# Gates of the last 128 tokens: three bf16 products per token in place of one fp32 product

## The chip, the cores and the metric

The kernel runs on one core of a Trainium2 chip. The metric is the device time of one execution in microseconds (us), taken as the median over several runs. Engines are named as the profile names them: PE is TensorE's matmul side and PEld its weight loads, DVE is VectorE, ACT is ScalarE, POOL is GpSimd, SP is SyncE, which here only issues transfers (SPq).

## What is computed

The program is a decoder trunk of four layers over 256 tokens of width 1024, all in fp32. Each layer has an attention mixer (sliding window, dilated, latent, sliding window again) and then an expert mixer, called PEER, with a normalisation behind each. PEER is where the change lies. Cut to what matters, it is this:

```
q     = x @ w_q                                   # 8 heads, two halves of 128
sc    = q . keys                                  # 128 keys per half
best, idx = top 16 of the sums of the top 16 of both halves   # idx = 128*row + column
gate  = softmax(best)                             # 16 experts per head, 8 heads
h     = gelu(x . u[idx]);  y = sum(gate * h * v[idx])
```

There are 128*128 experts, and each token uses 128 of them. The kernel does not gather rows of u and v. It computes gelu(x . u) for all 16384 experts as dense products, multiplies with a gate matrix that is zero for experts that a token did not choose, and multiplies with all of v.

## The kernel before

A layer's PEER stage has four parts, each bound to the stream of weights that SP loads in chunks of 512 KB (`raw`), ACT rounds to a high part (`hi`) and DVE, now and then POOL, subtracts to a low part (`lo`). Every large product is three fp32r products, hi*zh, lo*zh and hi*zl.

- Scores: `peer_scores` computes the queries and the key scores of 256 tokens on PE.
- Top-k: `topk_gen` runs as a side program on DVE, a few instructions per chunk, for tokens 0 to 127 first and then for tokens 128 to 255.
- The u phase: 128 chunks of u (index j), 24 products of 256 columns each on PE (`hp`, L141), followed by a gelu on ACT into G.
- The v phase: 123 chunks of v and five more at the end, 12 products of 512 columns each (L151 to L155), which read G after it has been multiplied by the gates and split.

The gates come by two ways. For tokens 0 to 127, POOL scatters them with 128 indirect transfers per layer (`scatter`, L957, `gates<-gt`) into a gate matrix in DRAM. SP fetches it piece by piece (L1022, `gt<-gates`) at the start of the v phase, after the last scatter has landed, and DVE multiplies it into G (L1031, `gated`). For tokens 128 to 255 the gate matrix is made on the chip. `topk_gen` ends with three fp32 transposes (L910) that turn row number, column number and gate value of each chosen expert into `tab`, with the 128 experts on the partitions and the tokens along the free axis. Then `weights_gen` takes the tokens in 32 units of four. For a unit, DVE builds in the tile `wk` a one-hot matrix over rows and one over columns (L925, both in one instruction of 1024 elements) and multiplies the second by the gate values (L927, 512 elements). PE multiplies the two for each token (L941, fp32, 128 x 128 x 128), which gives that token's 128 x 128 gate matrix in a bank of PSUM (`y0` to `y3`). `keep` then stores it into G (ACT, L999) or multiplies it into what stands there already (DVE, L1006).

The order of PE, DVE, ACT and SP is the order in which the code is written; POOL runs its scatters on its own. `pace` lets the side program run along the u phase: every chunk j gives it a budget, each `yield` takes the number behind it from the budget, and a unit of `weights_gen` costs 1. The units start when `topk_gen` has ended, with a budget per chunk of 35/(125 - j), so that they are spread over the rest of the u phase. Within a unit's step, the next unit's builds are issued on DVE ahead of this unit's products on PE.

The tile `wk` has two buffers and `sm` (the small PSUM tile that the transposes write) two.

Of the kernel before, what the change touches and what calls it, by code (L numbers as in the profile page):

```python
# [11 lines left out]
F32 = mybir.dt.float32  # L12
F32R = mybir.dt.float32r
BF = mybir.dt.bfloat16
# [3 lines left out]
OP = mybir.AluOpType  # L18
# [26 lines left out]
class Kernel:  # L45
# [453 lines left out]
    def swa(self, j):  # L499
        nc = self.nc  # L500
        self.turned = 1
        kT, vT = self.carve(T), self.carve(T)
        v = self.carve(2, 128)
        qTs = self.ring(8, T)
        pts = self.ring(4, 384)
        ptTs = self.ring(4, 384)
        st = self.ring(2, 6, 4)
        ost = self.carve(8, T)
        sk = self.carve(16)
        sinks = self.a["sinks"]  # L510
        nc.sync.dma_start(sk, bass.AP(tensor=sinks.tensor, offset=sinks.offset + 16 * j, ap=[[0, 128], [1, 16]]))
        self.xproj(kT, True)
        self.xproj(vT, True)
        self.vtrans(vT, v)
        bias = self.aux[:, 0:4096].rearrange("p (h s) -> p h s", h=16)

        def sink(c, s):
            sv = s.rearrange("p a (e t) -> p a e t", e=2)
            skc = sk[:, 2 * c:2 * c + 2][:, :, None].to_broadcast([128, 2, 2])
            nc.vector.tensor_add(sv[:, 2], sv[:, 0], skc)  # L520
            nc.vector.tensor_scalar(s[:, 2], s[:, 2], 88.0, None, op0=OP.min)
            nc.scalar.activation(s[:, 3], s[:, 2], AF.Exp)

        def gains(it):
            s = it["s"]
            nc.vector.tensor_add(s[:, 4], s[:, 3], s[:, 1])
            nc.vector.reciprocal(s[:, 5], s[:, 4])

        items = [dict(c=c, heads=(c, c + 8), s=st[c % 2], ix=[(0, 1), (2, 3)], pt=pts[2 * (c % 2):][:2],
                      ptT=ptTs[2 * (c % 2):][:2], v=v, scale=HD ** -0.5, bias=lambda h: bias[:, h, :],  # L530
                      terms=lambda e, c=c: [(qTs[c], kT, slice(64 * e, 64 * e + 64))]) for c in range(8)]
        ahead = 1 if self.started else 2
        for c in range(ahead):
            self.xproj(qTs[c])
        if not self.started:
            first = self.layers[0]
            todo = self.to_mask
            self.load_biases(first, nc.sync, slice(2, 4))
            self.to_mask = todo
            self.load_norms(first - 1, nc.sync)  # L540

        def after(c):
            sink(c, st[c % 2])

        def before(c):
            if ahead <= c + 1 < 8:
                self.xproj(qTs[c + 1])
            if c == 5 and not self.started:
                self.started = True

        if not self.started:
            self.mask_biases(2)
        self.pipeline(items, gains, ost, before, lambda c: self.mask_biases(2) if c else None, after)

    def dilated(self, j):
# [234 lines left out]
    def topk_gen(self, ids, val, tab, ready):  # L790


        nc = self.nc
        V = nc.vector
        svs, sis = self.ring(2, 16, 16), self.ring(2, 16, 16, dt=U32)
# [7 lines left out]
        stk = self.carve(3, 128)  # L803
# [15 lines left out]
        for t in range(2):  # L819
# [33 lines left out]
            shape = [128, 4, 16, 16]  # L853
# [54 lines left out]
        p = self.small((128, 4, 128))  # L908
        for q in range(3):
            nc.tensor.transpose(p[:, q, :], stk[:, q, :], self.ident)  # L910
        V.tensor_copy(tab, p[:, 0:3, :])
        yield 0.55

    def weights_gen(self, tab, keep):


        nc = self.nc
        V = nc.vector
        shape = [128, 2, 4, 128]
        units = {}  # L920

        def build(u):
            ts = slice(124 - 4 * u, 128 - 4 * u)
            ab = self.misc.tile(shape, F32, name="wk", bufs=2)
            V.tensor_tensor(ab, self.iota[:, None, None, :].to_broadcast(shape),  # L925
                            tab[:, 0:2, ts][:, :, :, None].to_broadcast(shape), op=OP.is_equal)
            V.tensor_mul(ab[:, 1], ab[:, 1], tab[:, 2, ts][:, :, None].to_broadcast([128, 4, 128]))  # L927
            units[u] = ab

        build(0)  # L930
        yield 1
        kept, due = None, None
        for u in range(34):
            if u + 1 < 32:
                build(u + 1)
            p = None
            if u < 32:
                p = self.ps.tile([128, 4, 128], F32, name=f"y{u % 4}", bufs=1)
                ab = units.pop(u)
                for k in range(4):  # L940
                    nc.tensor.matmul(p[:, k, :], ab[:, 0, k, :], ab[:, 1, k, :], start=True, stop=True)  # L941
            if due is not None:
                due()
            due = keep(256 - 4 * u, kept.rearrange("p t j -> p j t")) if kept is not None else None
            kept = p
            yield 1
# [26 lines left out]
    def peer(self, i, turn):  # L973
        nc = self.nc
        self.new_work()
        iv = self.misc.tile([128, 2, 128], F32, name="gt", bufs=2)
        ids, val = iv[:, 0, :].bitcast(I32), iv[:, 1, :]
        tab = self.misc.tile([128, 3, 128], F32, name="tab", bufs=1)
        self.sc = self.carve(2, 16, 128)
        self.sc_ready, self.paced = 0, 0.0  # L980
        sent = []
# [34 lines left out]
        rows = self.gates[i].rearrange("(n b p c) o -> n p b (c o)", b=2, p=128, c=128)  # L1016
# [64 lines left out]
        for j in range(n):  # L1081
# [12 lines left out]
            if j in (68, 71, 74, 77):  # L1094
                k = (j - 68) // 3
                self.load_norms(i, nc.sync, slice(k, k + 1))
            if j in (80, 83, 86, 89):
                k = (j - 80) // 3
# [79 lines left out]
    def setup(self):  # L1178
        nc, a = self.nc, self.a
        self.ident = self.misc.tile([128, 128], F32, name="ident", bufs=1)  # L1180
        nc.scalar.dma_start(self.ident, a["ident"])
        self.x = self.misc.tile([128, 2, 1024], F32, name="x", bufs=1)
        self.new_work()
        rb, oh, rr = self.carve(16), self.carve(RW), self.carve(RW)
        for t in range(2):
            nc.sync.dma_start(self.x[:, t, :], a["x"][t * 128:t * 128 + 128, :])
            if t == 0:
                nc.sync.dma_start(oh[0:32], a["bucket"])
        nc.scalar.dma_start(rb[0:32], a["rel_bias"])
        for _ in range(2):  # L1190
            self._load()
        self.eps = self.misc.tile([128, 4], F32, name="eps", bufs=1)
        nc.vector.memset(self.eps[:, 0:1], LN_EPS)
        nc.vector.memset(self.eps[:, 1:2], RMS_EPS)
        p = self.small()
        nc.tensor.matmul(p[0:16, 0:RW], rb[0:32], oh[0:32], start=True, stop=True)
        nc.scalar.activation(rr[0:16], p[0:16, 0:RW], AF.Copy, scale=HD ** 0.5)
        self.relb = self.dram.tile([16, RW], F32, name="relb")
        nc.sync.dma_start(self.relb, rr[0:16])
        self.prefetch()  # L1200
        self.new_z()
        for t in range(2):
            self.turn_lo(self.turn_hi(t, [self.asmall() for _ in range(2)]))
            self.split_to(0)
        self.prefetch()
        self.masks = self.misc.tile([128, 1024], F32, name="masks", bufs=1)
        nc.sync.dma_start(self.masks, a["masks"])
        self.new_aux()
        self.load_biases(self.layers[0], nc.sync, slice(0, 2))
        self.zero = self.misc.tile([128, 128], F32, name="zero", bufs=1)  # L1210
        nc.vector.memset(self.zero, 0.0)
        self.steps = self.misc.tile([128, 33], F32, name="steps", bufs=1)
        nc.gpsimd.dma_start(self.steps, a["steps"])
        self.iota = self.misc.tile([128, 128], F32, name="iota", bufs=1)
        nc.gpsimd.dma_start(self.iota, a["iota"])

    def build(self):
        tc = self.tc
# [114 lines left out]
```

## Time and profile before

| | |
|---|---|
| median of three runs | 3824.62 us (3823.56 to 3825.99) |
| the profiled execution | 3826.61 us, its span 3824.8 us, mean granted TensorE clock 0.999 |
| PE busy | 3792.5 us, 99% of the span |
| PEld, DVE, ACT, POOL busy | 91%, 74%, 49%, 29% |
| POOL's scatters, L957 | 1017.6 us in 512 instructions |

The span runs from the first to the last instruction; the time of the execution is 1.8 us longer. A duration of one PE or PEld instruction in the profile is longer than its share of the engine's time, since the instructions overlap: the share is read from the distance of two starts. Each fp32 product of L941 stands in the profile as two MATMUL records, so a unit of four products is eight records.

### The profile page before, as it was taken

The numbers are of one execution on the slowest core, as the hardware profiler recorded it, in microseconds if no ns is written. First come the engines' busy times: TensorE is split into PE (matmuls) and PEld (weight loads), VectorE is DVE, ScalarE is ACT, GpSimd is POOL, SyncE is SP. The second block draws the span as 40 slices with busy tenths as digits, with TensorE's granted clock in tenths as the row PEclk, the third lists the DMA queues.
The fourth block names the chain that finished last, engine by engine and source line by source line (L and its number), as shares of the span: only waits on it lengthen the run. The fifth ranks groups of instructions, "written<-read, shape, count | busy, mean of one in ns | idle before, by whom it ended". The sixth has DMA issues, their size and how long they took to land. (4 is left out here: it accounts for less than half of the span.)

```text
span 3824.8 us, 67261 instructions
## 1 busy us (share of the span) xinstructions
PE 3792.5 (99%) x25652; PEld 3468.1 (91%) x25652; DVE 2826.6 (74%) x5914; ACT 1878.3 (49%) x3400; POOL 1091.9 (29%) x548
## 2 busy tenths in 40 slices
PE   8999999999999999999999999999999999999999
PEld 7999998888998999988887999998888899998887
DVE  7787776676667887766667788776677788776666
ACT  5544444545554544455555444444555554445554
POOL 0158750000000188720000148860000128780000
PEclk9999999999999999999999999999999999999999
DMA  7667777775444577777762567778775456666665
GB/s 236 201 183 180 174 207 239 246 242 163 142 138 147 171 186 178 176 226 240 250 211 99 168 182 180 177 185 246 245 249 164 144 182 179 160 158 215 215 226 176
DMA packets 400996, 735.35 MB, mean 192 GB/s; under 512 B 102608, under 2 KB 240400, under 8 KB 400160
## 3 DMA queue, kind: packets, MB, share of 16 engines
q1 hardware_dynamic: 326688, 730.60, 59.4%
q0 software_dynamic: 73792, 0.38, 5.5%
q8 instruction: 201, 3.29, 0.3%
q14 instruction: 123, 1.01, 0.1%
q10 hardware_dynamic: 192, 0.07, 0.0%
HBM read 696.01 MB, written 34.89 MB: 191 GB/s over the span
## 5 line engine op out<-in xcount | busy, mean ns | idle before, releaser
L97 DVE TENSOR_TENSOR lo<-raw,hi 128x1024 fp32r<-128x1024 f32 x1182 | 1444.2, 1223 | 595.2 <-ACT hi L91 591.9
L91 ACT ACTIVATE hi<-raw 128x1024 fp32r<-128x1024 f32 x1212 | 1271.2, 1050 | 32.9 <-DMA raw<-in_peer_v 21.2
L957 POOL DMA_INDIRECT gates<-gt x512 | 1017.6, 1988 | 485.0 <-DVE G L808 247.7
L141 PE MATMUL hp<-zh,hi 128*128 128x256 f32 x5312 | 764.0, 286 | 1.6 <-ACT zh L242 0.7
L141 PE MATMUL hp<-zh,lo 128*128 128x256 f32 x5312 | 746.4, 283 | 0.0
L141 PE MATMUL hp<-zl,hi 128*128 128x256 f32 x5312 | 746.1, 283 | 0.0
L141 PEld LDWEIGHTS hp<-zh,hi 128*128 128x128 f32 x5312 | 682.7, 192 | 7.6 <-issue 4.5
L141 PEld LDWEIGHTS hp<-zh,lo 128*128 128x128 f32 x5312 | 685.9, 192 | 0.0
L141 PEld LDWEIGHTS hp<-zl,hi 128*128 128x128 f32 x5312 | 685.8, 192 | 0.0
L155 PE MATMUL y<-hi,wk 128*128 128x512 f32 x2004 | 624.9, 393 | 1.5 <-DVE wk L1037 1.3
L153 PE MATMUL y<-lo,wk 128*128 128x512 f32 x2004 | 623.1, 392 | 0.0
L151 PE MATMUL y<-hi,wk 128*128 128x512 f32 x2004 | 621.1, 390 | 0.0
L97 POOL TENSOR_TENSOR lo<-raw,hi 128x1024 fp32r<-128x1024 f32 x30 | 72.7, 2424 | 1871.8 <-ACT hi L91 1871.8
L1051 ACT ACTIVATE G<-hp 128x256 f32<-128x256 f32 (+26 forms) x512 | 182.6, 357 | 836.8 <-PE hp L141 825.9
L1036 ACT ACTIVATE wk<-G 128x256 fp32r<-128x256 f32 x492 | 205.9, 418 | 656.9 <-issue 625.1
L155 PEld LDWEIGHTS y<-hi,wk 128*128 128x128 f32 x2004 | 375.9, 188 | 85.5 <-DVE wk L1037 2.1
L151 PEld LDWEIGHTS y<-hi,wk 128*128 128x128 f32 x2004 | 375.8, 188 | 84.2 <-ACT wk L1113 0.3
L153 PEld LDWEIGHTS y<-lo,wk 128*128 128x128 f32 x2004 | 376.5, 188 | 80.1
L1037 DVE TENSOR_TENSOR wk<-G,wk 128x256 fp32r<-128x256 f32 x492 | 208.8, 424 | 263.3 <-ACT wk L1036 263.2
L427 ACT ACTIVATE G<-hp 128x256 f32<-128x256 f32 x156 | 59.7, 382 | 203.4 <-PE hp L141 195.9
L925 DVE TENSOR_TENSOR wk<-iota,tab 128x1024 f32<-128x1024 f32 x128 | 156.1, 1219 | 0.0
L1031 DVE TENSOR_TENSOR G<-G,gt 128x128 f32<-128x128 f32 x512 | 144.3, 284 | 7.6 <-DMA gt<-gates 7.4
(202 smaller groups left out, 2611.7 us busy)
## 6 DMA issues: line engine op xcount, KB each, us to landing
raw<-in_peer_u SPq DMA_DIRECT2D x512, 512.0 KB
raw<-in_peer_v SPq DMA_DIRECT2D x512, 512.0 KB
raw<-in_dil_w SPq DMA_DIRECT2D x72, 512.0 KB
gates<-zero SPq DMA_DIRECT2D x256, 128.0 KB
raw<-in_peer_wq SPq DMA_DIRECT2D x64, 512.0 KB
gt<-gates SPq DMA_DIRECT2D x256, 128.0 KB
raw<-in_swa_w SPq DMA_DIRECT2D x20, 512.0 KB
G<-in_lnp SPq DMA_DIRECT2D x16, 512.0 KB
```

Source lines behind the costliest of these rows:

```text
L91: nc.scalar.activation(h[:, :w], r[:, :w], AF.Copy)
L97: eng.tensor_sub(lo[:, :w], r[:, :w], h.bitcast(F32)[:, :w])
L141: mm(ps, w[:, k, :], z[:, k0 + k, :], start=(p == 0 and k == 0), stop=(p == 2 and k == nk - 1))
L151: mm(ps[t][b][:, :s.stop - s.start], zh[:, ts], hi[:, s], start=first, stop=False)
L153: mm(ps[t][b][:, :s.stop - s.start], zh[:, ts], lo[:, s], start=False, stop=False)
L155: mm(ps[t][b][:, :s.stop - s.start], zl[:, ts], hi[:, s], start=False, stop=last)
L925: V.tensor_tensor(ab, self.iota[:, None, None, :].to_broadcast(shape), tab[:, 0:2, ts][:, :, :, None].to_broadcast(shape), op=OP.is_equal)
L957: ins = self.nc.gpsimd.indirect_dma_start(self.gates[i], IndirectOffsetOnAxis(ap=ids[:, k:k + 1], axis=0), val[:, k:k + 1], None, compute_ ...
L1031: nc.vector.tensor_mul(g, g, gts[j // 2][:, j % 2, :])
L1036: nc.scalar.activation(gz[:, 0, :], g, AF.Copy)
L1037: nc.vector.tensor_sub(gz[:, 1, :], g, gz.bitcast(F32)[:, 0, :])
L1051: nc.scalar.activation(g[:, 0:td], ps[:, 0:td], AF.Gelu)
```

## The change

The one-hot matrices become bf16. The gate value is split into three bf16 parts, which together hold the fp32 value: `topk_gen` gains two subtractions and two casts for that, each with a `yield` of 0.28, and `tab` becomes bf16 with five rows. Row numbers and column numbers are whole numbers below 128. A unit's builds are now three DVE instructions. One compares a new constant `iota4` (each number 0 to 127 four times) with the column numbers, 512 elements in the order column, token. One multiplies that by the three parts of the gate, 1536 elements. One builds the rows' one-hot, 512 elements in the order token, row. PE computes three bf16 products per token, which add up in PSUM; the moving operand is read with a step of four elements, the stationary one without a step. `iota4` is made by one DVE instruction in the first layer's mixer.

```
+                nc.vector.tensor_copy(self.iota4, self.iota[:, :, None].to_broadcast([128, 128, 4]))
                 self.started = True
...
-        V.tensor_copy(tab, p[:, 0:3, :])
+        V.tensor_copy(tab[:, 0:3], p[:, 0:3, :])
         yield 0.55
+        left = stk[:, 0, :]
+        V.tensor_sub(left, p[:, 2, :], tab[:, 2])
+        yield 0.28
+        V.tensor_copy(tab[:, 3], left)
+        yield 0.28
+        V.tensor_sub(left, left, tab[:, 3])
+        yield 0.28
+        V.tensor_copy(tab[:, 4], left)
+        yield 0.28
...
-            ab = self.misc.tile(shape, F32, name="wk", bufs=2)
-            V.tensor_tensor(ab, self.iota[:, None, None, :].to_broadcast(shape),
-                            tab[:, 0:2, ts][:, :, :, None].to_broadcast(shape), op=OP.is_equal)
-            V.tensor_mul(ab[:, 1], ab[:, 1], tab[:, 2, ts][:, :, None].to_broadcast([128, 4, 128]))
-            units[u] = ab
+            ab = self.misc.tile([128, 2048], BF, name="wk", bufs=2)
+            rows = ab[:, 0:512].rearrange("p (k i) -> p k i", k=4)
+            cols = ab[:, 512:2048].rearrange("p (q j k) -> p q j k", q=3, k=4)
+            V.tensor_tensor(cols[:, 2], self.iota4, tab[:, 1, ts][:, None, :].to_broadcast([128, 128, 4]),
+                            op=OP.is_equal)
+            V.tensor_mul(cols, cols[:, 2][:, None].to_broadcast([128, 3, 128, 4]),
+                         tab[:, 2:5, ts][:, :, None, :].to_broadcast([128, 3, 128, 4]))
+            V.tensor_tensor(rows, self.iota4[:, :, 0][:, None, :].to_broadcast([128, 4, 128]),
+                            tab[:, 0, ts][:, :, None].to_broadcast([128, 4, 128]), op=OP.is_equal)
+            units[u] = rows, cols
...
-                    nc.tensor.matmul(p[:, k, :], ab[:, 0, k, :], ab[:, 1, k, :], start=True, stop=True)
+                    for q in range(3):
+                        nc.tensor.matmul(p[:, k, :], rows[:, k, :], cols[:, q, :, k], start=q == 0, stop=q == 2)
...
-        tab = self.misc.tile([128, 3, 128], F32, name="tab", bufs=1)
+        tab = self.misc.tile([128, 5, 128], BF, name="tab", bufs=1)
```

On PE, in the first layer, around the first unit of four tokens (L941, tile `y_4218`), the kernel before has this order; `hp` is the u phase's product:

```order
L141 MATMUL hp<-zl,hi 128x256 x8
L141 MATMUL hp<-zh,hi 128x256 x8
L141 MATMUL hp<-zh,lo 128x256 x8
L141 MATMUL hp<-zl,hi 128x256 x8
L941 MATMUL y_4218<-wk 128x128 x4
L141 MATMUL hp<-zh,hi 128x256 x8
```

At the same place, one chunk later, the changed kernel has this (L957 is now the line of the products, the tile is `y_4259`):

```order
L141 MATMUL hp<-zl,hi 128x256 x8
L957 LDWEIGHTS wk
L957 MATMUL y_4259<-wk 128x128
L957 LDWEIGHTS wk
L957 MATMUL y_4259<-wk 128x128
```

Four fp32 products, which load their weights themselves, became twelve pairs of a load and a product. Counted over a layer, the 32 units stood behind chunks 2, 4, 6, 8, 9 and so on to 58 after the transposes, and stand now behind chunks 3, 5, 7, 9, 10 and so on to 58.

On DVE, in the first layer, between the copy of the transposes (L911) and the second unit's builds, before; `lo` is the low part of a weight chunk:

```order
L911 COPY tab<-sm 128x384
L97 TENSOR_TENSOR lo<-raw,hi 128x1024
L925 TENSOR_TENSOR wk<-iota,tab 128x1024
L927 TENSOR_TENSOR wk<-wk,tab 128x512
L97 TENSOR_TENSOR lo<-raw,hi 128x1024
L925 TENSOR_TENSOR wk<-iota,tab 128x1024
L927 TENSOR_TENSOR wk<-wk,tab 128x512
```

And now, where the copy is L913, the parts of the gate L916 to L922 and the three builds L937, L939 and L941:

```order
L913 CAST tab<-sm 128x384
L916 TENSOR_TENSOR G_1091<-sm,tab 128x128
L918 CAST tab<-G_1091 128x128
L920 TENSOR_TENSOR G_1091<-G_1091,tab 128x128
L922 CAST tab<-G_1091 128x128
L97 TENSOR_TENSOR lo<-raw,hi 128x1024 x2
L937 TENSOR_TENSOR wk<-iota_140,tab 128x512
L939 TENSOR_TENSOR wk<-wk,tab 128x1536
L941 TENSOR_TENSOR wk<-iota_140,tab 128x512
```

Four small instructions stand behind the copy, the first build comes behind two `lo` instead of one, and each unit has three instructions instead of two. The copy to `iota4` stands in the first layer's mixer, on DVE between a `lo` and the score reductions (L330) of the sixth of eight pairs of heads.

## Rows read from the trace of the kernel before

**Rows 1.** The page, part 1: busy us, share of the span, count, by engine.

```profile
PE 3792.5 (99%) x25652; PEld 3468.1 (91%) x25652; DVE 2826.6 (74%) x5914; ACT 1878.3 (49%) x3400; POOL 1091.9 (29%) x548
```

**Rows 2.** Waits of PE, one of 18 groups: us in total, times, longest us.

```profile
PE y L155 <- DVE wk L1037: 1.3, 1, 1.3
```

**Rows 3.** The chain that ended last, fourth layer: start us, us, what.

```profile
3009.22 1.74 PE hp L434 x16
...
3248.46 5.76 PE hp L141 x48
3254.21 0.89 PE y L941 x8
3255.10 5.75 PE hp L141 x48
```

**Rows 4.** Groups by line and form: out<-in, shapes, count, busy us, mean ns, idle before.

```profile
L925 DVE TENSOR_TENSOR wk<-iota,tab 128x1024 f32<-128x1024 f32 x128 | 156.1, 1219 | 0.0
L1031 DVE TENSOR_TENSOR G<-G,gt 128x128 f32<-128x128 f32 x512 | 144.3, 284 | 7.6 <-DMA gt<-gates 7.4
...
L941 PEld LDWEIGHTS y<-wk 128*128 128x128 f32 x1024 | 125.4, 191 | 0.0
...
L927 DVE TENSOR_TENSOR wk<-wk,tab 128x512 f32<-128x512 f32 x128 | 88.6, 692 | 4.4
...
L357 PEld LDWEIGHTS y<-G 128*64 128x64 f32 x264 | 16.0, 136 | 9.5 <-issue 2.5
...
L879 DVE TENSOR_TENSOR G<-G 128x1024 bf16<-128x1024 bf16 x16 | 10.9, 684 | 0.0
...
L406 PEld LDWEIGHTS sm<-ident,G 128*128 128x128 f32 x52 | 6.2, 141 | 2.0 <-ACT G L427 2.0
```

**Rows 5.** Timeline of PE, v phase of layer four: start us, us, what.

```profile
3600.28 0.62 PE L153 MATMUL y<-lo,wk 128*128 128x512 f32 x2
3600.74 0.62 PE L155 MATMUL y<-hi,wk 128*128 128x512 f32 x2
```

**Rows 6.** Window of the 32 units, layer four: busy us (count) by engine.

```profile
3248.00:3444.00 196.00, 196.00 (x1656) 196.00 (x1655) 151.05 (x237) 86.79 (x204) 157.34 (x85) 1.00 0.66 159
```

**Rows 7.** Timeline of POOL and DVE, u phase of layer four.

```profile
3282.68 1.55 POOL L957 DMA_INDIRECT gates<-gt  x1 [0.30 <-issue]
...
3283.15 1.23 DVE L97 TENSOR_TENSOR lo<-raw,hi 128x1024 fp32r<-128x1024 f32 x1 [2.12 <-ACT hi L91]
...
3284.38 1.22 DVE L925 TENSOR_TENSOR wk<-iota,tab 128x1024 f32<-128x1024 f32 x1
...
3284.53 2.49 POOL L957 DMA_INDIRECT gates<-gt  x1 [0.30 <-issue]
...
3286.66 1.22 DVE L97 TENSOR_TENSOR lo<-raw,hi 128x1024 fp32r<-128x1024 f32 x1
...
3287.32 1.98 POOL L957 DMA_INDIRECT gates<-gt  x1 [0.30 <-issue]
```

**Rows 8.** Timeline: each layer's last scatter and first v product.

```profile
534.94 1.55 POOL L957 DMA_INDIRECT gates<-gt  x1 [0.30 <-issue]
...
548.71 0.62 PE L151 MATMUL y<-hi,wk 128*128 128x512 f32 x2
...
1647.71 1.55 POOL L957 DMA_INDIRECT gates<-gt  x1 [0.31 <-issue]
...
1663.35 0.62 PE L151 MATMUL y<-hi,wk 128*128 128x512 f32 x2
...
2561.43 2.50 POOL L957 DMA_INDIRECT gates<-gt  x1 [0.30 <-issue]
...
2571.17 0.65 PE L151 MATMUL y<-hi,wk 128*128 128x512 f32 x2
...
3448.24 1.55 POOL L957 DMA_INDIRECT gates<-gt  x1 [0.30 <-issue]
...
3463.86 0.62 PE L151 MATMUL y<-hi,wk 128*128 128x512 f32 x2
```

More of the change, by code (lines that the diff above doesn't have):

```diff
@@ L918, in weights_gen @@
         V = nc.vector
-        shape = [128, 2, 4, 128]
         units = {}
@@ L938, in weights_gen @@
                 p = self.ps.tile([128, 4, 128], F32, name=f"y{u % 4}", bufs=1)
-                ab = units.pop(u)
+                rows, cols = units.pop(u)
                 for k in range(4):
-                    nc.tensor.matmul(p[:, k, :], ab[:, 0, k, :], ab[:, 1, k, :], start=True, stop=True)
+                    for q in range(3):
+                        nc.tensor.matmul(p[:, k, :], rows[:, k, :], cols[:, q, :, k], start=q == 0, stop=q == 2)
             if due is not None:
@@ L1215, in setup @@
         nc.gpsimd.dma_start(self.iota, a["iota"])
+        self.iota4 = self.misc.tile([128, 128, 4], BF, name="iota4", bufs=1)
     def build(self):
```

## The prediction

> **What bounds the kernel now.** I read the page's busy shares first, then PE's waits, the chain that ended last, the groups by form, and last the timeline around the stage. PE is busy for 99% of the span [rows 1], and its only wait in the expert mixers is 1.3 us [rows 2]; the other 17 groups of PE's waits lie in the program's start, the attention stages and the normalisations. So PE sets the time, and an edit is worth what it takes from PE, as long as what PE waits for keeps up. The chain shows how the edited work lies in it: 48 products of the u phase, then eight records of L941 for 0.89 us, then the next 48 [rows 3]. A unit of four tokens stands on the path with its whole 0.89 us. There are 32 units in each of four layers: 128 * 0.89 = 114 us, 3.0% of the span. That is all the change can touch on PE.
>
> **PE: eight records out, twelve pairs of load and product in.** An L941 record now takes 0.89/8 = 111 ns. The new pair, one pass over 128 bf16 columns, is in no row, so I bound it. In the v phase two products of 512 columns start 0.46 us after the two before, 230 ns each [rows 5]; a u product of 256 columns takes 5.76/48 = 120 ns [rows 3]. The slope is 110/256 = 0.43 ns per column, and the straight line through both ends at 65 ns for 128 columns. The columns alone would be 128 * 0.43 = 55 ns. If an fp32 record is two such passes (110 ns), its 111 leaves about 1 ns for the rest, and a single pass would be 56. From above, the dearest row is the present record, 111 ns. So the pair lies between 55 and 111. I take 61, halfway between 56 and the line's 65, because both come from products that follow each other without a gap, as the new ones will. Break-even is 890/12 = 74 ns.
>
> What speaks against 61 is the weight load. The profile's load of 128 columns lasts 191 ns and one of 64 columns 136 [rows 4]: 55 ns more for 64 columns, so 110 ns for 128 and some 81 fixed. And L434, a single-pass product of only 128 columns, still takes 1.74/16 = 109 ns [rows 3], as if the load set it. What speaks for 61: the loads before the transposes (L406), also 128 columns, last 141 [rows 4], 60 ns without the fixed part. A load of 128 columns can go at about half the price, and 60 ns would hide behind 61.
>
> The Trainium skill ("TensorE: Matmul & The Clock Gate", section "Weight-path perf modes") says that a load of exactly 128 weights in a type other than fp32 goes in a fast mode, measured at about twice the rate. No row here has a bf16 load; half of 110 would be 55 ns, and the sum by it is the one made here.
>
> With 61 a unit takes 12 * 0.061 = 0.73 us and saves 0.158; a layer saves 32 * 0.158 = 5.1 us.
>
> **DVE: beside PE, covered.** The builds cost 1.219 + 0.692 = 1.91 us per unit [rows 4]. By L1031 (128 elements, 284 ns), L927 (512, 692) and L925 (1024, 1219), an instruction with one element per cycle takes about 150 + 1.04 ns per element. L879, bf16 in and out with a repeated operand, takes 684 ns for 1024, which is 150 + 0.52 per element. At that rate the new compare of 512 is 417 and the product of 1536 is 951; the rows' one-hot, which repeats one element along the innermost axis, I leave at 692. Together 2.06 us, 0.15 more, 4.8 us per layer. The four instructions that split the gate are 4 * 0.284 = 1.1 us. DVE is busy 151 of the stage's 196 us [rows 6], so 6 us more hide in 45 us of idle time. What stands behind the builds on DVE is the next `lo`, which PE needs two chunks later, so a late build is not felt at once. The later first unit (chunk 3 for 2) moves no work out of the stage.
>
> **The copy to `iota4`** is once 512 elements: between 0 and 0.69 us (L927) on PE's path, in an attention stage where PE does wait for DVE. The sixth pair of heads lies ahead of the stage's worst waits; I take 0.3.
>
> **POOL: the deadline behind the stage.** The v phase cannot begin before the last scatter has landed and been fetched. From the end of the last scatter to the first v product the layers show 548.71 - 536.49 = 12.2, 14.1, 7.2 and 14.1 us [rows 8]. In the third, PE just does not wait at its first v product and stalls 1.3 us soon after [rows 2], so 7.2 us is what the way from scatter to product needs; the others have 5.0, 6.8 and 6.8 us to spare. A saving of 5.1 us per layer fits into these; in the third layer it would run into POOL.
>
> POOL's own pace hangs on DVE, however. A scatter takes 1.55 us when no long DVE instruction runs at its start (the one at 3282.68 starts ahead of L97). The one at 3284.53 starts inside L925, which ends at 3285.60, and ends at 3287.02; the one at 3287.32 starts inside L97, which ends at 3287.88, and ends at 3289.30 [rows 7]. Both end 1.42 us after the DVE instruction: it holds the scatter until it is through. DVE follows PE's chunks, so when PE gets faster the holds end earlier too, and three instructions of at most 0.95 us hold a scatter for less than one of 1.22. So POOL also ends earlier, by an amount that I bound by 0 and the whole saving. For the third layer I take half: 2.5 us.
>
> **Sum.** Layers one, two and four save 5.1 each, the third 2.5, less 0.3: 17.5 us. From the profiled execution's 3826.6 us (span 3824.8 and 1.8 around it) that gives 3809.1. The median of the runs is 2.0 lower than the profiled execution, so the forecast for the median is 3807.1, say 3807. Its own range: at 55 ns a unit saves 0.23 and a layer 7.4, of which layer one can use 5.0 if POOL stays where it is, and the third 3 to 4: about 25 us, 3800. At 69 ns a layer saves 2.0: 8 us, 3817.
>
> **Rivals.**
> - *The load stays at full price.* Each pair takes what every 128-column product takes now, 109 to 111 ns, L434's price. A unit is 12 * 0.111 = 1.33 us, 0.44 more; 128 units are 56.6 us: 3882 us. It decides as soon as a pair passes 74 ns. For it: every product of 128 columns in the trace. Against it: L406's load. A moving operand that is read at half rate for its step of four elements would cost the same (2 * 55 ns); no row has such a step.
> - *The load is fast but half of it sticks out.* 55 ns of columns and half of L406's 60 are 85 ns: 1.02 us per unit, 0.13 more, 16.6 us: 3842 us. For it: the u product has 120 ns for columns that need 110 by the slope, so load and product are not wholly apart. The Trainium skill (same page, section "Back-to-back issue gap") gives 81 ns for such a stream of load and product at 128 columns; by it a unit is 0.97 us and the time 3835. No row here shows it.
> - *DVE's multiplication runs at one element per cycle.* Then it is 150 + 1.04 * 1536 = 1.75 us and the compare 0.69, the builds 3.13 us: 39 us more per layer, and DVE has 151 + 39 + 1 = 191 us of work in a stage of 191. PE would wait for `lo` as often as it gains: about 3824 us. Against it: L879; but its inner run is 16 elements, the new one 4.
> - *POOL does not follow.* The new builds meet the scatters in another phase. About 85 scatters start in a stage [rows 6]; 0.1 us more hold for each is 8.5 us, which eats the spare time and the saving of three layers: about 3824 us. Against it: shorter builds.
>
> **Chances.** Forecast 0.64, full price 0.13, half of the load 0.10, DVE 0.07, POOL 0.06. About 0.2%, 7.6 us, is what a measurement can tell here from no change. Faster than that: all but 0.02 of the forecast's 0.64 and 0.01 from DVE and POOL, 0.63. Slower: full price, half of the load, and 0.02 of DVE and POOL, 0.25. Within: 0.12. The range from 3796 to 3843 holds the forecast, DVE, POOL and most of the half-load case, and leaves out full price.
>
> **What the profile after would show.** The eight records of 0.89 us in the chain become 24 instructions of about 0.73 us; 0.97 to 1.02 would be the half-load case, 1.3 the full price. The bf16 loads would last near 140 ns, not 191. The builds would read about 0.42, 0.95 and 0.69 us; 1.75 in the middle is the DVE case. From the last scatter's end to the first v product the first, second and fourth layers should keep more than 7.2 us. If the third layer still waits for its gates and the other three do not, the sum over the layers is right. I am wrong on the step that matters most if the pair is above 74 ns, however well the rest fits.

## The result and the profile after

The changed kernel takes 3889.17 us (median of four runs, 3887.98 to 3889.67) against 3824.92 us for the kernel before in the same session (3823.56 to 3825.99). The ratio is 1.0168 with an interval of 1.0155 to 1.0180: slower by 64 us. The prediction was 3807 us, faster by 17 us, with a range up to 3843.

The page of the changed kernel, part 1, answers to [rows 1]: busy us, share of the span, instructions.

```profile
PE 3854.4 (99%) x26164; PEld 3526.2 (91%) x26164; DVE 2840.8 (73%) x6055; ACT 1877.3 (48%) x3396; POOL 1024.2 (26%) x548
```

PE has 62 us more of busy time and still fills 99% of the span. DVE has 14 us more, POOL 68 less. So the loss is work on PE, or what counts as such in the profile, and not a new wait.

The chain that ended last, fourth layer, answers to [rows 3]: start us, us, what.

```profile
3303.35 1.39 PE y L957 x12
3304.74 5.75 PE hp L141 x48
3310.50 1.40 PE y L957 x12
3311.89 5.75 PE hp L141 x48
```

The 48 u products between two units take what they took before, 5.75 us. A unit takes 1.40 us where it took 0.89. That is 0.51 us more, 32 times per layer: 16.3 us. The next lines show that this is all. They are the timeline of the changed kernel's fourth layer: the transposes that open the stage, the last scatter, and the first v product.

```profile
3294.24 0.49 PE L912 MATMUL sm<-ident,G 128*128 128x128 f32 x3
...
3477.19 1.55 POOL L973 DMA_INDIRECT gates<-gt  x1 [0.30 <-issue]
...
3526.13 0.62 PE L151 MATMUL y<-hi,wk 128*128 128x512 f32 x2
```

From the transposes to the first v product it is 3526.13 - 3294.24 = 231.9 us. In the kernel before it was 215.9 us in every layer. The difference, 16.0 us, is the same in all four layers, and four times 16.0 is the 64 us of the result. The last scatter now ends 47.4 us ahead of the first v product, not 14.1 [rows 8]: POOL is far from setting anything here.

The groups by form answer to [rows 4]: out<-in, shapes, count, busy us, mean ns, idle before.

```profile
L957 PE MATMUL y<-wk 128*128 128x128 bf16 x1536 | 198.8, 294 | 0.0
L957 PEld LDWEIGHTS <-wk 128*128 128x128 bf16 x1536 | 161.0, 113 | 6.0
L939 DVE TENSOR_TENSOR wk<-wk,tab 128x1536 bf16<-128x1536 bf16 x128 | 122.7, 958 | 4.4
L941 DVE TENSOR_TENSOR wk<-iota,tab 128x512 bf16<-128x512 bf16 x128 | 87.5, 683 | 0.0
L937 DVE TENSOR_TENSOR wk<-iota,tab 128x512 bf16<-128x512 bf16 x128 | 53.5, 418 | 0.0
```

DVE's builds take 418, 958 and 683 ns, close to the 417, 951 and 692 of the prediction. The load takes 113 ns, not the 191 of the fp32 load, so it is even cheaper than the 140 that was hoped for. And yet a pair of load and product takes 1.40/12 = 116 ns. PE's waits show none on `wk` or on the gates; the 1.3 us of [rows 2] is gone.

The window of the 32 units answers to [rows 6]: busy us (count) of PE, PEld, DVE, ACT and POOL, then granted clock, DMA share, GB/s.

```profile
3294.00:3506.00 212.00, 212.00 (x1784) 210.50 (x1783) 154.36 (x272) 87.02 (x203) 146.82 (x88) 1.00 0.64 148
```

The clock is full and DVE is idle for 58 of 212 us. Something inside the pair doubles its price, and nothing around it shows what.

### The profile page after: what moved, and what is told of

The parts are those of the page before. It is cut to its first block, busy times and chain, and to the rows that moved or that the text cites. A ratio compares the mean times of both kernels' runs of the same rounds, so it can differ in the third digit from the quotient of the medians.

```text
span 3887.1 us, 68417 instructions
## 1 busy us (share of the span) xinstructions
PE 3854.4 (99%) x26164; PEld 3526.2 (91%) x26164; DVE 2840.8 (73%) x6055; ACT 1877.3 (48%) x3396; POOL 1024.2 (26%) x548
## 4 chain that ended last, share of the span: by engine, by line
PE 96%; DVE 2%; ACT 1%; DMA 0%; issue 0%; SPq 0%; ACTq 0%; DVEq 0%
PE hp L141 49%; PE y L155 13%; PE y L153 13%; PE y L151 13%; PE y L957 5%; PE sm L778 1%; PE sm L323 1%; DVE lo L97 1%; PE hp L434 1%; PE y L357 0%; PE sm L237 0%; DVE G L330 0%; PE hp L357 0%; PE sm L225 0%; PE sm L350 0%
## 5 line engine op out<-in xcount | busy, mean ns | idle before, releaser
L973 POOL DMA_INDIRECT gates<-gt x512 | 950.0, 1856 | 484.1 <-DVE G L810 247.7
L1053 DVE TENSOR_TENSOR wk<-G,wk 128x256 fp32r<-128x256 f32 x492 | 208.7, 424 | 262.4 <-ACT wk L1052 262.2
L957 PE MATMUL y<-wk 128*128 128x128 bf16 x1536 | 198.8, 294 | 0.0
L957 PEld LDWEIGHTS <-wk 128*128 128x128 bf16 x1536 | 161.0, 113 | 6.0
```

What stands on the lines that cost most here:

```text
L957: nc.tensor.matmul(p[:, k, :], rows[:, k, :], cols[:, q, :, k], start=q == 0, stop=q == 2)
L973: ins = self.nc.gpsimd.indirect_dma_start(self.gates[i], IndirectOffsetOnAxis(ap=ids[:, k:k + 1], axis=0), val[:, k:k + 1], None, compute_ ...
L1053: nc.vector.tensor_sub(gz[:, 1, :], g, gz.bitcast(F32)[:, 0, :])
```

## The experiments

Four theories were named. LOAD: the weight load sets 116 ns. STEP: PE reads the moving operand at half rate, because its columns lie four bf16 elements, 8 bytes, apart. ADD: three products in a row into the same columns of PSUM wait for each other. DEADLINE, for the rest of the sum: once the units are as cheap as forecast, the scatters to the gate matrix end too late and take part of the gain back.

**The step alone.** `e1_contig` keeps everything and builds the columns token by token, so that each product reads 128 contiguous elements.

```
-            cols = ab[:, 512:2048].rearrange("p (q j k) -> p q j k", q=3, k=4)
+            cols = ab[:, 512:2048].rearrange("p (q k j) -> p q k j", q=3, k=4)
...  # compare and product run over [4, 128] in place of [128, 4]
-   nc.tensor.matmul(p[:, k, :], rows[:, k, :], cols[:, q, :, k], start=q == 0, stop=q == 2)
+   nc.tensor.matmul(p[:, k, :], rows[:, k, :], cols[:, q, k, :], start=q == 0, stop=q == 2)
```

> The columns' one-hot is laid out token by token, so the moving operand is read without a step; everything else of the change stays. Pair of bf16 load and product in the changed kernel: 1.40/12 = 117 ns. Theory STEP (the step of four elements halves the rate at which the moving operand is read: 2*55 ns and some): the pair falls to 55-65 ns, a unit to 0.66-0.78 us. Theory LOAD (the short bf16 load, some 60 ns, is not hidden behind the 55 ns of columns): the pair stays at 115-117 ns, a unit at 1.40. Theory ADD (three products in a row add into the same PSUM columns and wait for each other): stays at 115-117. The builds on DVE lose their fast form (0.69+1.75+0.69 = 3.13 us per unit in place of 2.06), so DVE is about full in the stage and the total may not fall as far as PE's own work: STEP 3805-3830 us, LOAD and ADD 3885-3895.

It took 3815.59 us against 3827.07 (ratio 0.9973, 0.9949 to 0.9998). The groups by form of this kernel:

```profile
L939 DVE TENSOR_TENSOR wk<-wk,tab 128x1536 bf16<-128x1536 bf16 x128 | 225.1, 1759 | 4.4
...
L957 PE MATMUL y<-wk 128*128 128x128 bf16 x1536 | 107.9, 220 | 1.2 <-DVE wk L941 1.2
...
L957 PEld LDWEIGHTS <-wk 128*128 128x128 bf16 x1536 | 86.0, 98 | 7.8 <-DVE wk L941 2.0
```

Starts of two pairs lie 55 to 56 ns apart (median), half of 116, with the same loads and the same additions in PSUM. STEP holds. The price moved to DVE: with the gate repeated along the innermost axis the product of 1536 takes 1759 ns, not 958. The gain is smaller than 116 to 55 ns would make it, because of the gates. The chain of this kernel, around the same place in the fourth layer, no longer runs over PE:

```profile
3256.11 2.56 DMA gates<-gt
3258.67 3.47 issue
```

It runs over the scatters. From the last scatter to the first v product the layers had 4.5, 11.1, 5.5 and 4.5 us, and PE waited for its first v operands, 2.8 us in the first layer and 1.0 in the third, and another 3.2 us in three waits soon behind the first products.

**The additions alone.** `e2_qouter` keeps the step and changes the order, so that consecutive products go to different tokens.

```
-                for k in range(4):
-                    for q in range(3):
-                        nc.tensor.matmul(p[:, k, :], rows[:, k, :], cols[:, q, :, k], start=q == 0, stop=q == 2)
+                for q in range(3):
+                    for k in range(4):
+                        nc.tensor.matmul(p[:, k, :], rows[:, k, :], cols[:, q, :, k], start=q + k == 0, stop=q == 2,
+                                         skip_group_check=True)
```

> The twelve products of a unit in another order: first part of all four tokens, then the second, then the third, so that no two products in a row add into the same PSUM columns. ADD: the pair falls from 117 ns to about 60. STEP and LOAD: 115-117 ns, time 3886-3891 us.

One run took 3888.18 us. The chain of this kernel:

```profile
3302.69 1.40 PE y L957 x12
3304.09 5.75 PE hp L141 x48
```

The unit is 1.40 us as before the swap. ADD falls.

**A step of two.** `e3_step2` interleaves the columns by two tokens, with two compares of 256 and two products of 768 on DVE.

```
+            cols = ab[:, 512:2048].rearrange("p (u q j k) -> p u q j k", u=2, q=3, k=2)
...
-   nc.tensor.matmul(..., cols[:, q, :, k], ...)
+   nc.tensor.matmul(..., cols[:, k // 2, q, :, k % 2], ...)
```

> Columns interleaved by two tokens instead of four (a step of two elements in the moving operand). STEP: if the loss grows with the step, the pair lies between 61 and 117 ns, at 61 if two neighbours come with one read; if any step costs the same, 117. LOAD and ADD: 115-117 ns. DVE's builds are about 2*(0.28+0.55)+0.69 = 2.4 us.

One run took 3816.17 us. Its chain in the fourth layer:

```profile
3257.91 0.71 PE y L959 x12
3258.61 5.79 PE hp L141 x48
```

A pair takes 57 to 58 ns: a step of 4 bytes is nearly free, while DVE keeps its short instructions. From transposes to v products the last three layers take 211.2 to 211.4 us, 4.5 to 4.7 below the kernel before, and the first takes 214.2. There the gates are late. The timeline of POOL and PE of this kernel, end of the first layer's u phase (in brackets the idle time before and what ended it):

```profile
540.36 2.58 POOL L975 DMA_INDIRECT gates<-gt  x1 [0.30 <-issue]
...
547.43 1.22 PE L151 MATMUL y<-hi,wk 128*128 128x512 f32 x2 [2.85 <-ACT wk L1054]
```

The last scatter ends at 542.94, and 4.5 us later PE starts, after 2.85 us of waiting for an operand that needs the gates. This is the wait that DEADLINE names. In the second layer the last scatter also ends 4.5 us ahead. PE gets its first v operands in time there, and waits behind the first products, as its timeline shows:

```profile
1663.69 0.73 PE L151 MATMUL y<-hi,wk 128*128 128x512 f32 x2 [0.59 <-ACT wk L1054]
...
1666.32 0.95 PE L155 MATMUL y<-hi,wk 128*128 128x512 f32 x2 [1.45 <-DVE wk L1055]
```

In the third and fourth layers the last scatter ends 14.7 us ahead, and PE waits for no gates.

**The load alone.** `e4_wide` issues one load and one product of 384 contiguous columns per token, so that each load serves three times the columns. The three parts of the gate are not added up in it.

```
-            cols = ab[:, 512:2048].rearrange("p (q j k) -> p q j k", q=3, k=4)
+            cols = ab[:, 512:2048].rearrange("p (k q j) -> p q k j", q=3, k=4)
...  # compare and product run over [4, 128], as in e1_contig
-                    for q in range(3):
-                        nc.tensor.matmul(p[:, k, :], rows[:, k, :], cols[:, q, :, k], start=q == 0, stop=q == 2)
+                    nc.tensor.matmul(p[:, min(k, 1):min(k, 1) + 3, :], rows[:, k, :], cols[:, :, k, :],
+                                     start=True, stop=True, skip_group_check=True)
```

> Leaves out the adding of the three parts: one product per token with 384 columns in a row, no step, so four loads and four products per unit in place of twelve; the gates of the last 128 tokens are then not computed rightly. Columns alone are 384*0.43 = 165 ns. STEP: the load hides, a pair takes 166-178 ns, a unit 0.67-0.71 us. LOAD: the load of some 60 ns adds to the columns, 225 ns, a unit 0.90 us. ADD says nothing here (no adding): 0.67-0.71.

One run took 3813.7 us. The groups by form:

```profile
L956 PE MATMUL y<-wk 128*128 128x384 bf16 x512 | 105.4, 329 | 4.5 <-DVE wk L941 4.2
...
L956 PEld LDWEIGHTS <-wk 128*128 128x128 bf16 x512 | 39.7, 98 | 28.7 <-DVE wk L941 6.9
```

Two starts lie 162 to 163 ns apart (median): 0.42 ns per column, about as in the pairs of 55 ns with 128 columns each. From the start of one unit to the next, with 48 u products between, it is 6.41 us here and 6.49 in `e1_contig`. Eight loads and products less per unit saved 0.08 us, 10 ns for each, where LOAD needs some 60. LOAD falls.

**A step in the stationary operand.** `e5_rows4` uses the step of two for the columns (one compare of 512, two products of 768) and interleaves the rows by four tokens.

```
-            rows = ab[:, 0:512].rearrange("p (k i) -> p k i", k=4)
+            rows = ab[:, 0:512].rearrange("p (i k) -> p i k", k=4)
```

> Columns interleaved by two tokens as in the run with a step of two (58 ns per pair, a unit 0.71 us), and now the rows' one-hot too is interleaved, by four: the stationary operand is loaded with a step of four elements, which lets DVE build it at two elements per cycle (0.42 in place of 0.69 us). If a step of four halves the load's rate as it does the moving operand's, the load takes up to twice some 60 ns and the pair rises to 80-117 ns. If the load does not mind the step, the pair stays at 58-60 ns and the time at 3812-3818 us, DVE's builds falling from 2.4 to 0.42+2*0.56+0.42 = 2.0 us.

It took 3813.17 us against 3825.64 (ratio 0.9969, 0.9952 to 0.9987). Its chain, and from its groups by form the load:

```profile
3245.89 0.74 PE y L958 x12
3246.64 5.80 PE hp L141 x48
```

```profile
L958 PEld LDWEIGHTS <-wk 128*128 128x128 bf16 x1536 | 95.0, 115 | 5.5
```

The load grows from 96 to 115 ns, and the median pair from 58 to 60. A unit and the 48 u products behind it take 6.54 us, for 6.50 in `e3_step2`, which is 3 ns per pair. The same step that doubles the price in the moving operand costs 2 to 4 ns in the stationary one.

This kernel has no wait of PE on the gates, although its scatters start when those of `e3_step2` do. Its last scatter ends 11.2 us ahead in the first layer and 15.8 in the others. What differs on DVE are the builds, 1.95 us per unit in place of 2.37.

**The deadline.** `v1_early` is the step of two with one compare, and makes the first half of the top-k run faster, so that the scatters begin earlier. `v0_early` does only the latter, to the kernel before. The edit that both share:

```
-            self.pace(2.0)
+            self.pace(2.3)
...
-            self.pool_share = 0.0 if t else 0.4
+            self.pool_share = 0.0 if t else 0.6
...
-                rate = 2.0 if self.pool_share else 1.6
+                rate = 2.3 if self.pool_share else 1.6
```

> Columns interleaved by two tokens, and the scatters of the first 128 tokens begin earlier: the budget of the first top-k is 2.3 per chunk in place of 2.0, and POOL takes 0.6 of the low parts in that stretch in place of 0.4. Theory DEADLINE (with the fast pairs, what is saved on PE is lost where the v phase waits for the last scatter, 2.8 us in the first layer, and in the slow products behind that wait): scatters begin about 10 us earlier, the waits of the first v products go, and the time falls from 3816 to 3803-3808 us. Theory BUILDS (the loss against 32*(0.89-0.71)*4 = 23 us lies in DVE's builds, not in the gates): no gain from an earlier scatter, 3812-3818.

> The kernel before with the same earlier scatters and nothing else. It tells what of the last run is the earlier scatter alone. In the kernel before only the third layer is short of time (1.3 us of waiting): 3822-3825 us if nothing else changes; more if DVE or POOL is overfull in the stretch of the first top-k.

`v1_early` took 3806.3 us against 3825.64 (ratio 0.9943, 0.9925 to 0.9961), the best kernel of this study. `v0_early` took 3825.09 (0.9996, 0.9986 to 1.0006): in the kernel before, the earlier scatters are worth nothing. The chain of `v1_early` in the fourth layer, and then its timeline there:

```profile
3247.55 0.71 PE y L959 x12
3248.26 5.79 PE hp L141 x48
```

```profile
3231.93 0.49 PE L912 MATMUL sm<-ident,G 128*128 128x128 f32 x3
...
3423.94 1.55 POOL L975 DMA_INDIRECT gates<-gt  x1 [0.30 <-issue]
...
3443.14 0.62 PE L151 MATMUL y<-hi,wk 128*128 128x512 f32 x2
```

From transposes to v products it is now 211.2 us in every layer, the first among them, and the last scatter ends 15.8 to 17.6 us ahead. No wait of PE on the gates is left. The gain of 4.7 us in four layers is 18.8 of the 19.3 us measured. But `v1_early` also has one compare where `e3_step2` has two, so the 10 us between them are not shown to come from the scatters' edit alone: in `e5_rows4` the waits went with shorter builds and without it. Two runs that differ in this edit alone stand at the end of this section.

**fp32 with a step.** `e6_fp32step2` is the kernel before with its fp32 columns interleaved by two, again a step of 8 bytes.

```
+            cols = ab[:, 1].rearrange("p a b -> p (a b)").rearrange("p (u j k) -> p u j k", u=2, k=2)
...
-   nc.tensor.matmul(p[:, k, :], ab[:, 0, k, :], ab[:, 1, k, :], start=True, stop=True)
+   nc.tensor.matmul(p[:, k, :], ab[:, 0, k, :], cols[:, k // 2, :, k % 2], start=True, stop=True)
```

> The kernel before, fp32 products, with its columns interleaved by two tokens: a step of two elements of 4 bytes, 8 bytes as in the changed kernel's four elements of 2. If bytes decide, the moving operand is read at half rate: a record goes from 111 to about 220 ns, a unit from 0.89 to 1.7-1.8 us, the time to 3930-3945 us. If the step in elements decides (two is free in bf16), the unit stays at 0.89 us and the time at 3825-3832.

One run took 3827.02 us. Its chain:

```profile
3254.43 0.91 PE y L945 x8
3255.34 5.75 PE hp L141 x48
```

A record takes 112 to 114 ns where it took 111, so 8 bytes per column don't double an fp32 record. That fits a record that already spends 110 ns on its 128 columns, if it reads each of them once. Whether it does was not tried.

**Other steps.** `e7_step3` and `e7_step8` read the columns with a step of 3 and of 8 elements from wherever these fall in `wk`.

```
-            units[u] = rows, cols
+            units[u] = rows, ab      # cols below is the whole tile
...
-   nc.tensor.matmul(..., cols[:, q, :, k], ...)
+   nc.tensor.matmul(..., cols[:, 512 + 384 * q + k:512 + 384 * q + 382 + k:3], ...)   # e7_step3
+   nc.tensor.matmul(..., cols[:, 512 * q + k:512 * q + 1017 + k:8], ...)              # e7_step8
```

> The changed kernel with its builds, but each product reads its 128 moving columns with a step of three bf16 elements (6 bytes) from the same tile; the gates of the last 128 tokens are then not computed rightly. Steps of one, two and four gave 55, 58 and 116 ns. LINEAR (the loss grows with the bytes passed over, beyond 4 per column): 6/4 of 55 and some, 80-90 ns, a unit about 1.0 us, time about 3838. CLIFF (any step of more than two elements costs the double): 116 ns, a unit 1.40 us, 3889 us. LINE (what counts is how many columns come from one stretch of 16 bytes, 2.7 here, 2 at a step of four): between the two, about 80-90, not told from LINEAR by this run.

> The same with a step of eight elements (16 bytes); the gates of the last 128 tokens are again not computed rightly. LINEAR and LINE: 220-230 ns per pair, a unit 2.7 us, time about 4055. CLIFF: 116 ns, a unit 1.40 us, 3889.

Both keep the changed kernel's builds, so that only PE's reading differs; what they multiply are not the gates. They took 3848.87 and 4120.03 us, one run each. The chain of the step of 3, and then that of the step of 8:

```profile
3273.48 1.06 PE y L957 x12
3274.54 5.77 PE hp L141 x48
```

```profile
3475.80 2.72 PE y L957 x12
3478.53 5.75 PE hp L141 x48
```

The price rises with the bytes from one column to the next: a step of 3 elements costs less than one of 4, so CLIFF falls, and one of 8 costs twice as much as one of 4. LINEAR and LINE give the same prices at these steps and are not told apart. The prices of all steps:

| step | bytes per column | unit | pair | bytes per ns |
|---|---|---|---|---|
| 1 (`v2_contig_early`) | 2 | 0.69 us | 55 ns | 4.7 |
| 2 (`v1_early`) | 4 | 0.71 us | 58 ns | 8.8 |
| 3 (`e7_step3`) | 6 | 1.06 us | 84 to 88 ns | 8.7 to 9.1 |
| 4 (the change) | 8 | 1.40 us | 116 ns | 8.8 |
| 8 (`e7_step8`) | 16 | 2.72 us | 226 ns | 9.1 |

(The last column is 128 columns times their bytes by the pair.) Up to 4 bytes the columns set the price, 55 ns; beyond, it is about 9 bytes per ns of stretch read through.

**No step, with the deadline moved.** `v2_contig_early` is `e1_contig` with the earlier scatters.

> Columns without a step (56 ns per pair) and the earlier scatters. Against the columns interleaved by two with earlier scatters (3806 us): PE's unit is 12*2 = 0.03 us shorter, 4 us in all, but DVE's builds take 3.15 us per unit in place of 2.2, 30 us more per layer, and DVE then has some 190 of the stage's 190 us to do. If DVE holds, 3802-3806 us; if PE waits for it or POOL's scatters are held longer by builds of 1.75 us, 3808-3815.

It took 3807.55 us against 3828.95 (ratio 0.9944, 0.9926 to 0.9961), no different from `v1_early`. Its chain and a window over its units in the fourth layer:

```profile
3242.43 0.77 PE y L957 x12
3243.19 5.79 PE hp L141 x48
3248.99 0.69 PE y L957 x12
```

```profile
3242.00:3438.00 196.00, 195.69 (x1821) 194.08 (x1820) 187.20 (x275) 88.91 (x209) 152.57 (x83) 1.00 0.67 161
```

The first unit of the layer takes 0.77 us since it waits for its builds for a moment; from then on a DVE that is busy for 187 of 196 us holds nobody up. Against `e1_contig` only the edit to the scatters differs, and 8 us came back. The intervals of the two overlap, but the traces agree: from transposes to v products the layers took 214.5, 211.3, 212.4 and 211.5 us and now take 211.2 to 211.3, and PE's 7.0 us of waits for v operands became 0.9. So late gates did cost this time.

How the edit did it is only in part in its name. The first scatter starts 111.8 us ahead of the transposes where it was 109.7, just 2.1 us earlier. The last scatter, counted from the transposes, ends earlier by 11.8, 1.9, 8.7 and 8.6 us, 31 us in all. Half of that is scatters that take less time, 15 us in the four layers, as the groups of `e1_contig` and then of this kernel show:

```profile
L973 POOL DMA_INDIRECT gates<-gt x512 | 1014.1, 1981 | 496.6 <-DVE G L810 247.7 <-issue 186.4 <-DMA gates<-gt 62.5
```

```profile
L973 POOL DMA_INDIRECT gates<-gt x512 | 999.2, 1951 | 471.8 <-DVE G L810 230.7 <-issue 187.7 <-DMA gates<-gt 53.5
```

Of the 512 scatters 359 take more than 1.7 us in `e1_contig` and 338 here. [rows 7] show such scatters end behind an instruction of DVE, so these meet DVE at other moments; whether they do so because they start earlier was not tested.

## Why the prediction was wrong

**What bounds the kernel: right.** Every microsecond of a unit stood on the path. 0.51 us more in 128 units is 65 us, and the loss is 64.

**The pair of 61 ns: wrong, and this step alone decides.** The prediction took 61 "because both come from products that follow each other without a gap, as the new ones will". The rows were read well for what they show: without a step a pair takes 55 to 56 ns, a step of two 57 to 58, both inside the 55 to 65 of the estimate. But the products of [rows 3, 5] read contiguous columns, and the new ones don't; the section on the change even says that the moving operand is read with a step of four. The number belonged to another access pattern. The bound from above failed with it: 111 ns was the dearest row of 128 columns that it took, and 116 is above it. The right case stood in one sentence, "a moving operand that is read at half rate for its step of four elements would cost the same", and was put aside because no row had such a step. The lack of a row is a reason for a rival with a chance of its own, not against it.

**The rival at 3882 us: near in time, wrong in mechanism.** Full price of the load gives 111 ns and 3882, the step 116 ns and 3889. The load had nothing to do with it: it took 113 ns with the step of four, and 98 in `e4_wide`, where it was hidden behind 162 to 163 ns of columns. The Trainium skill ("TensorE: Matmul & The Clock Gate", section "Weight-path perf modes"), which the prediction weighed, names about twice the rate for such loads; the traces agree, with 96 to 98 ns against 191 for fp32.

**Half of the load sticks out: wrong.** It wanted 85 ns per pair. Without a step the pair takes 55. The 81 ns that the Trainium skill gives for such a stream (same page, section "Back-to-back issue gap") are not reached here; the measurement decides.

**DVE: right in the changed kernel, and its rival was priced too high.** The builds are 2.06 us as worked out. The multiplication at one element per cycle, which the rival feared, came true in `e1_contig` and `v2_contig_early` with 1759 ns, where the prediction had 1.75 us. It had PE wait for `lo` and all of the gain lost, at 3824 us. `v2_contig_early` is at 3807.55: PE waits for builds for 0.9 us in the whole program and for `lo` not at all. 9 us of idle time in 196 were enough. The prediction's own remark, that PE needs a `lo` only two chunks later, would explain it, but no run tests that.

**POOL's deadline: right in kind, its place and size off.** In the changed kernel it could not be seen, since PE became slower. With pairs of 58 ns the gates came late as forecast, but in the first and second layers and not in the third (`e3_step2`), and the way from scatter to product is 4.5 us where the prediction read 7.2 from a layer that it took for tight. The hold that the prediction read from two scatters is the common case: in the kernel before, 332 of the 512 start inside a DVE instruction with two inputs, and 90% of these end 1.40 to 1.45 us behind it. But that POOL follows a faster PE does not hold in each layer. Counted from the transposes, the last scatter ends 215.9 - 12.2 = 203.7 us behind them in the first layer of the kernel before [rows 8] and 214.2 - 4.5 = 209.7 in that of `e3_step2`, so later; in the third it is 208.7 and 196.5, so earlier. The rival "POOL does not follow" was right for two of four layers: from one layer's transposes to the next's `e3_step2` takes 5.6 and 5.1 us more than `v1_early` in the first two, and the same within 0.3 us in the others. That is the 10 us between 3816 and 3806, and about half of the gain.

**The sum.** With another layout of `wk` and gates that are not late, the time is 3806.3 us (`v1_early`), and the forecast was 3807. That they meet so closely is in part luck. A unit saves about 0.15 us there, as forecast, but not because a pair takes 61 ns: it takes 58, and the 48 u products behind the unit lose 0.04 us (5.79 for 5.75). And all four layers save 4.7 us, where the forecast had 5.1 in three and 2.5 in one. With the scatters as they were, the same columns gave 3816 us in `e3_step2`. So beside the pair, POOL's term did not hold either. The 0.3 us for `iota4` was not measured by itself.

## What to carry to other kernels

Before you price a new product by rows of the trace, compare the access pattern of the moving operand as well as type and size: here a step of 8 bytes doubled it, a step of 4 bytes cost 3 ns of 55, and a step of 8 bytes in the stationary operand 2 to 4 ns. If a layout is wanted for DVE's sake, look for the one that both engines read well: interleaving by two kept DVE's product at 2*555 ns and PE's pair at 58. And when a stage is made shorter, look at what must be ready at its end: here PE stopped waiting for the gates only when the last scatter ended earlier, by an edit that was worth nothing before (`v1_early`; `v2_contig_early` but for 0.9 us) or by shorter builds (`e5_rows4`).

## What the runs showed of the hardware

A strided bf16 moving operand of 128 columns costs about 1 ns per 9 bytes of the stretch it spans, from 4 bytes per column on, up to the step of 16 bytes that was tried (table above). The Trainium skill ("SBUF — State Buffer", section "Specifications (TRN2)") says that two hits in a line of 16 bytes give full bandwidth; the step of four has two, and took twice the time, so for this read the measurement decides.

The granted clock can fall after a short wait. These are windows of `e3_step2` around the wait of 2.85 us in the first layer, in the columns of the window above:

```profile
535.00:544.00 9.00, 9.00 (x77) 9.00 (x77) 4.75 (x9) 3.23 (x8) 7.33 (x3) 1.00 0.47 100
547.40:550.60 3.20, 3.17 (x8) 2.52 (x9) 1.85 (x3) 2.62 (x5) 0.00 (x0) 0.51 0.84 287
550.60:553.00 2.40, 2.19 (x10) 1.46 (x8) 1.38 (x3) 1.37 (x2) 0.00 (x0) 1.00 0.96 294
```

PE was busy without a gap until the wait, at full clock. Behind it the granted clock was 0.51, the level of 1.2 GHz, for 3.2 us, and then full again. The same in PE's timeline, products of 512 columns in that stretch and after it:

```profile
548.45 1.05 PE L153 MATMUL y<-lo,wk 128*128 128x512 f32 x2
549.30 1.05 PE L155 MATMUL y<-hi,wk 128*128 128x512 f32 x2
...
550.78 0.62 PE L153 MATMUL y<-lo,wk 128*128 128x512 f32 x2
551.24 0.63 PE L155 MATMUL y<-hi,wk 128*128 128x512 f32 x2
```

Two products take 0.85 us from start to start at the lower level and 0.46 at the higher. The four pairs from 547.43 to 550.78 took 3.35 us, where four at the higher level take 1.84: the wait of 2.85 us cost 1.5 us more than its length. In the second layer of this run PE waited 0.59 and 1.45 us close together, and from 1666.7 to 1670.0 us the granted clock was 0.50, again the level of 1.2 GHz. The waits and this clock are most of the 5 us that `e3_step2` loses in each of the two layers.

In `e7_step8` the granted clock was below 1 while its units ran, though PE never waited there. A window of its fourth layer:

```profile
3470.00:3680.00 210.00, 210.00 (x1378) 178.62 (x1377) 118.86 (x208) 68.24 (x157) 151.79 (x86) 0.93 0.54 116
```

The run is 291 us slower than the kernel before (4120 against 3829), and 128 units of 2.72 us for 0.89 explain 234. The rest goes with this clock. In the stages with units it fell 40 times in the four layers, each time about 0.4 to 1.0 us behind the start of a unit's last product, and 48 u products with a fall among them take longer than 5.75 us in the chain:

```profile
3487.00 7.24 PE hp L141 x48
```

40 times 1.5 us is 60 us, about the 57 that are left. What in the units lowers the clock was not tested. The price of its pair is read from units in the chain between which the u products take the usual 5.75 us.
